# Weight sums of a seven-product matrix scheme: GpSimd differences of loaded tiles, or adding DMA transfers from DRAM

## The chip, the cores and the metric

The kernel runs on one core of a Trainium2 chip. The metric is the device time of one execution in microseconds (us), and a kernel is described by the median of its runs. A profiled execution gives a trace; times inside it are counted from the start of its span. In the traces PE is TensorE, DVE is VectorE, ACT is ScalarE, POOL is GpSimd and SP is SyncE, which here issues most of the DMA transfers.

## What is computed

One inference step of a transformer-like layer: a token mixer (attention and mLSTM) and then an MLP, for 640 tokens (512 latent and 128 context tokens) of width 1024. The change touches the MLP alone, and of it the first matrix:

```python
D_MODEL, D_FF = 1024, 4096

def trunk_layer(x, ...):
    ...
    x = x + gate1 * rmsnorm(mix, post1)
    h = rmsnorm(x, pre2) * (1 + scale2) + shift2
    ff = jnp.square(jax.nn.relu(h @ w_mlp1)) @ w_mlp2
    x = x + gate2 * rmsnorm(ff, post2)
```

All arithmetic is float32. On TensorE every product of two float32 matrices is made of three: each factor is split into a high and a low part (fp32r), and high x high, high x low and low x high are summed.

## The kernel before

Everything ahead of the MLP is left alone. The MLP works on transposed activations `h2`, 128 features by 640 tokens, eight such slabs. `w_mlp1` is cut into 32 blocks of 128 columns and `w_mlp2` accordingly; the loop `for ch in range(NCH)` takes four blocks a round. Chunk 0 makes plain products with tiles loaded early (`w0`). Chunks 1 to 7 take their four blocks as two pairs (`p`), and make h @ w_mlp1 for a pair with seven products in place of eight: the tokens are cut into two halves of 320, the 1024 features into two halves of 512, and the pair gives two column blocks. So the activations are a 2 x 2 block matrix A(i, j), the weights one of four quarters of 128 x 512 elements (256 KB), and a scheme of Strassen's kind needs sums of blocks on either side:

- the sums of the activation blocks, called S3 to S7 (`fac`, `parts`, L1055 to L1066), are made once, at the end of chunk 0, on DVE and GpSimd, and split into high and low parts by ACT and DVE;
- the sums of the weight quarters, made anew for each pair in `factors`. `raw_pair` loads both blocks (512 KB each) into the one tile `gate`. GpSimd makes from it `t13` and `t24`, two tiles of two quarters each (L845 to L849, four operations). They come from the pool entry `x2`, which has three buffers, so the second pair's `t24` reuses the buffer of the first pair's `t13` of the same chunk. `quarters` then splits a tile of two quarters into high and low parts: an ACT cast (L829) and a DVE subtraction (L830), into a ring of six weight tiles (`ring`) that also serves the `w_mlp2` tiles (`load_w`, L107 to L112). The lone fourth quarter goes into `mix` (L853, L854).

`pair` runs the products: the banks bY, bW and bV collect running sums, copied from bank to bank by ACT (L1009, L1015, L1022), and `squared` makes relu squared and splits the result into `uh` and `ul`, which the products with `w_mlp2` (L116 to L118, in `sums`) read.

The program is written in this order for each chunk, but a scheduler decides the order of the instructions on each engine, by a simulated timeline; each engine then works strictly in its order. `tc.issue_after(mark[...])` holds a group of instructions back in that planning until the marked one. All loads from DRAM here go through SP's queue, which waits at each transfer until its buffer is free; behind it the next transfers stand.

Of the kernel before, what the change touches and what calls it, by code (L numbers as in the profile page):

```python
# [26 lines left out]
def _build(ctx, tc, nc, a, dbg):  # L27
# [802 lines left out]
        V.tensor_tensor(out=lo, in0=x, in1=hi, op=ALU.subtract)  # L830
        return [[y.rearrange("p (q k n) -> p q k n", q=2, k=4)[:, q] for y in (hi, lo)] for q in range(2)]

    def raw_pair(src):
        raw = pR_.tile([P, 2, 1024], F32, name="gate")
        for n in range(2):
            nc.sync.dma_start(raw[:, n, :], src[n])
        return raw[:, 0, :], raw[:, 1, :]

    def factors(b1, b2, f):

        if 1 not in f:
            f[1], f[2] = quarters(b1)
        q1, q2 = ([b[:, 0:512], b[:, 512:1024]] for b in (b1, b2))
        t13 = pR_.tile([P, 1024], F32, name="x2", bufs=3)
        G.tensor_tensor(out=t13[:, 0:512], in0=q2[0], in1=q1[0], op=ALU.subtract)  # L845
        G.tensor_tensor(out=t13[:, 512:1024], in0=q2[1], in1=q2[0], op=ALU.subtract)
        t24 = pR_.tile([P, 1024], F32, name="x2", bufs=3)
        G.tensor_tensor(out=t24[:, 0:512], in0=q2[1], in1=t13[:, 0:512], op=ALU.subtract)
        G.tensor_tensor(out=t24[:, 512:1024], in0=q1[1], in1=t24[:, 0:512], op=ALU.subtract)  # L849

        v = pR_.tile([P, 1024], F32R, name="mix", bufs=2)
        hi, lo = v[:, 0:512], v[:, 512:1024]
        S.copy(hi, q2[1])  # L853
        V.tensor_tensor(out=lo, in0=q2[1], in1=hi, op=ALU.subtract)  # L854
        f[3] = [y.rearrange("p (k n) -> p k n", k=4) for y in (hi, lo)]

        def rest():
            f[5], f[7] = quarters(t13)
            f[6], f[4] = quarters(t24)
        return rest  # L860
# [129 lines left out]
    def squared(uh, ul, i, r=None, ps=None):  # L990

        c = slice(320 * i, 320 * i + 320)
        u = pF_.tile([P, 320], F32, name="u", bufs=2)
        if ps is not None:
            S.activation(out=u, in_=ps, func=AF.Relu)  # L995
            V.tensor_tensor(out=u, in0=u, in1=u, op=ALU.mult)  # L996
        else:
            V.scalar_tensor_tensor(out=u, in0=r, scalar=0.0, in1=r, op0=ALU.max, op1=ALU.mult)
        S.copy(uh[:, c], u)  # L999
        V.tensor_tensor(out=ul[:, c], in0=u, in1=uh[:, c], op=ALU.subtract)  # L1000

# [39 lines left out]
    for ch in range(NCH):  # L1041
        us = []
        if ch == 0:
            uu = [u_pair() for _ in range(2)]
            us = [(u[0][n], u[1][n]) for u in uu for n in range(2)]
            for hf in range(2):
                q = (f2[1], f2[2]) if hf == 0 else (f2[3], f2[4])
                for m in range(CH):
                    ps = bank1()[:, 0:320]
                    with tc.issue_after(mark["turn"]) if m == 3 and hf == 0 else ExitStack():  # L1050
                        for k in range(KD):
                            x = [y[:, k % 4, :] for y in q[k // 4]]
                            mm3(ps, w0[m][0][:, k, :], w0[m][1][:, k, :], *x, k == 0, k == KD - 1)
                    squared(*us[m], hf, ps=ps)
            for h, k in enumerate(ks):  # L1055
                V.tensor_tensor(out=s1[h], in0=A(1, 0)[:, k, :], in1=A(1, 1)[:, k, :], op=ALU.add)
                parts(5, h, s1[h])
            for h, k in enumerate(ks):
                mark["S2"] = G.tensor_tensor(out=s1[h], in0=s1[h], in1=A(0, 0)[:, k, :], op=ALU.subtract).ins
                parts(6, h, s1[h])  # L1060
            for h, k in enumerate(ks):
                G.tensor_tensor(out=A(1, 0)[:, k, :], in0=A(0, 0)[:, k, :], in1=A(1, 0)[:, k, :], op=ALU.subtract)
                parts(7, h, A(1, 0)[:, k, :])
            for h, k in enumerate(ks):
                V.tensor_tensor(out=A(0, 1)[:, k, :], in0=A(0, 1)[:, k, :], in1=s1[h], op=ALU.subtract)
                parts(3, h, A(0, 1)[:, k, :])  # L1066
        else:
            if ch == 1:
                weights(1, keep=1)
                banks(0, 5)  # L1070
                pfork = tc.tile_pool(name="pfork", bufs=1, space=bass.MemoryType.PSUM, reuse_waits="tile")
                pfork_ = pfork.__enter__()
                forks = [pfork_.tile([P, 512], F32, name="b" + s)[:, 0:320] for s in "YWV"]

                for b in forks:
                    prime(b)
            for p in range(2):
                n = ch * 2 + p
                f = {}
                with tc.issue_after(mark["S2"]) if n == 2 else ExitStack():  # L1080
                    rest = factors(*raw_pair(a["w_mlp1"][2 * n:2 * n + 2]), f)
                rest()
                u = u_pair()
                for _ in pair(f, False, u, [bank1()[:, 0:320] for _ in range(2)] + forks):
                    pass
                us += [(u[0][n], u[1][n]) for n in range(2)]
# [160 lines left out]
```

## Time and profile before

| | us |
|---|---|
| median of 3 runs (lowest, highest) | 1057.35 (1056.98, 1058.0) |
| profiled execution | 1055.42 |
| its span, first to last instruction | 1053.7 |
| PE busy in the span | 1022.7 (97%) |
| DVE, ACT, POOL busy | 561.0, 424.2, 238.1 |

Matmuls overlap their neighbours, so PE's busy share says that it hardly idled, not that it ran at its peak. The granted TensorE clock was 0.996 of full speed over the span. The page's cut into 40 slices shows TensorE at nine tenths or more in nearly all of them; the stretch in which the MLP begins, about 630 to 660 us, and the first and the last slice are the exceptions. The chain that ended last runs 89% through PE.

### The profile page before, as it was taken

The numbers are of one execution on the slowest core, as the hardware profiler recorded it, in microseconds if no ns is written. First come the engines' busy times: TensorE is split into PE (matmuls) and PEld (weight loads), VectorE is DVE, ScalarE is ACT, GpSimd is POOL, SyncE is SP. The second block draws the span as 40 slices with busy tenths as digits, with TensorE's granted clock in tenths as the row PEclk, the third lists the DMA queues.
The fourth block names the chain that finished last, engine by engine and source line by source line (L and its number), as shares of the span: only waits on it lengthen the run. The fifth ranks groups of instructions, "written<-read, shape, count | busy, mean of one in ns | idle before, by whom it ended". The sixth has DMA issues, their size and how long they took to land.

```text
span 1053.7 us, 15728 instructions
## 1 busy us (share of the span) xinstructions
PE 1022.7 (97%) x6342; PEld 907.0 (86%) x6342; DVE 561.0 (53%) x955; ACT 424.2 (40%) x784; POOL 238.1 (23%) x218
## 2 busy tenths in 40 slices
PE   4999999899999999999999998999999999999997
PEld 2899899888889888888888897898989898989896
DVE  4655255767664222222334489365566565656557
ACT  4354244277775222222223564442425152515142
POOL 3011225424560000001000015224040404040101
PEclk9999999999999999999999999999999999999999
DMA  9444132211002444444446251231313131313034
GB/s 372 168 129 145 46 109 73 75 41 41 15 8 79 139 143 140 141 140 141 140 141 223 77 180 62 79 121 40 120 40 120 40 120 41 121 41 121 1 111 169
DMA packets 40121, 112.03 MB, mean 106 GB/s; under 512 B 4280, under 2 KB 14168, under 8 KB 38768
## 3 DMA queue, kind: packets, MB, share of 16 engines
q1 hardware_dynamic: 34656, 92.92, 25.8%
q0 software_dynamic: 4672, 16.80, 4.9%
q10 hardware_dynamic: 720, 1.31, 0.3%
q8 instruction: 50, 0.82, 0.3%
q14 instruction: 23, 0.19, 0.1%
HBM read 105.03 MB, written 5.98 MB: 105 GB/s over the span
## 4 chain that ended last, share of the span: by engine, by line
PE 89%; DVE 5%; ACT 2%; issue 2%; DMA 1%; POOL 1%; SPq 0%; POOLq 0%; DVEq 0%; ACTq 0%
PE b L116 20%; PE b L117 20%; PE b L118 20%; PE b L937 7%; PE bY L937 5%; PE b L149 3%; PE bV L937 2%; PE bW L937 2%; PE b L695 2%; PE b L683 2%; PE b L229 1%; PE b L496 1%; PE b L470 1%; DMA x<-x 1%; DMA gate<-w_mlp 1%
## 5 line engine op out<-in xcount | busy, mean ns | idle before, releaser
L112 DVE TENSOR_TENSOR wl<-raw,wh 128x1024 fp32r<-128x1024 f32 (+2 forms) x67 | 80.5, 1202 | 157.7 <-ACT wh L111 156.4
L111 ACT CAST wh<-raw 128x1024 fp32r<-128x1024 f32 (+2 forms) x69 | 69.8, 1013 | 175.0 <-PE b L117 157.0
L117 PE MATMUL b<-h1l,wh 128*128 128x320 f32 x400 | 125.2, 313 | 0.0
L116 PE MATMUL b<-h1h,wh 128*128 128x320 f32 x384 | 119.9, 312 | 0.0
L118 PE MATMUL b<-h1h,wl 128*128 128x320 f32 x384 | 118.9, 310 | 0.0
L117 PEld LDWEIGHTS b<-h1l,wh 128*128 128x128 f32 x400 | 75.2, 188 | 6.9 <-issue 6.9
L116 PEld LDWEIGHTS b<-h1h,wh 128*128 128x128 f32 x384 | 72.2, 188 | 7.1 <-DVE sg L808 5.0
L845 POOL TENSOR_TENSOR x<-gate 128x512 f32<-128x512 f32 x14 | 19.7, 1406 | 235.2 <-DMA gate<-w_mlp 220.8
L118 PEld LDWEIGHTS b<-h1h,wl 128*128 128x128 f32 x384 | 72.2, 188 | 0.3 <-issue 0.2
L117 PE MATMUL b<-wlx,uh 128*128 128x512 f32 (+1 forms) x164 | 64.5, 393 | 2.4 <-DVE wlx L112 2.4
L116 PE MATMUL b<-whx,uh 128*128 128x512 f32 (+1 forms) x164 | 64.1, 395 | 1.6 <-ACT u L995 1.6
L1125 DVE TENSOR_TENSOR h1h<-h1h,b 128x512 f32<-128x512 f32 (+1 forms) x71 | 46.2, 673 | 35.8 <-PE b L118 35.6
L117 PE MATMUL b<-wl,uh 128*128 128x512 f32 x160 | 63.2, 395 | 0.0
L116 PE MATMUL b<-wh,uh 128*128 128x512 f32 x160 | 62.1, 396 | 0.0
L118 PE MATMUL b<-whx,ul 128*128 128x512 f32 (+1 forms) x164 | 61.5, 393 | 0.0
L118 PE MATMUL b<-wh,ul 128*128 128x512 f32 x160 | 60.4, 394 | 0.0
L742 POOL DMA_DIRECT2D aw<-w_ada x32 | 17.4, 545 | 185.8 <-PE b L149 178.6
L999 ACT CAST uh<-u 128x320 fp32r<-128x320 f32 x64 | 29.3, 459 | 74.4 <-DVE u L996 48.7
L612 POOL TENSOR_TENSOR pt<-pt,sm 128x640 f32<-128x640 f32 x32 | 40.0, 1255 | 46.7 <-DVE sm L610 44.5
L112 DVE TENSOR_TENSOR wlx<-raw,whx 128x1024 fp32r<-128x1024 f32 (+2 forms) x28 | 34.6, 1234 | 27.9 <-ACT whx L111 27.8
L149 PE MATMUL b<-aw,csil 128*32 128x256 f32 (+1 forms) x256 | 35.2, 519 | 6.4 <-DMA aw<-w_ada 6.4
L117 PEld LDWEIGHTS b<-wlx,uh 128*128 128x128 f32 x164 | 31.1, 190 | 9.6 <-DVE wlx L112 2.8
(432 smaller groups left out, 2812.8 us busy)
## 6 DMA issues: line engine op xcount, KB each, us to landing
raw<-w_mlp SPq DMA_DIRECT2D x36, 512.0 KB, 3.2
aw<-w_ada POOLq DMA_DIRECT2D x32, 512.0 KB, 4.2
gate<-w_mlp SPq DMA_DIRECT2D x28, 512.0 KB
aw<-w_ada SPq DMA_DIRECT2D x8, 1024.0 KB, 12.0
raw<-w_g SPq DMA_DIRECT2D x16, 512.0 KB, 5.3
x<-x SPq DMA_DIRECT2D x10, 512.0 KB, 8.0
raw<-w_y SPq DMA_DIRECT2D x8, 512.0 KB, 3.3
raw<-w_out SPq DMA_DIRECT2D x8, 512.0 KB, 4.3
```

Source lines behind the costliest of these rows:

```text
L111: S.copy(hi, raw)
L112: eng.tensor_tensor(out=lo, in0=raw, in1=hi, op=ALU.subtract)
L116: T.matmul(out, lh, rh, start=start, stop=False)
L117: T.matmul(out, lh, rl, start=False, stop=False)
L118: T.matmul(out, ll, rh, start=False, stop=stop)
L149: T.matmul(ps[32 * j:32 * j + 32, 0:n], csil[:, k, :], raws[k], start=k < 4, stop=k >= 4, tile_position=(0, 32 * j))
L612: G.tensor_tensor(out=pt, in0=pt, in1=sm.broadcast_to([P, 640]), op=ALU.mult)
L683: T.transpose(pp[:, j * 128:(j + 1) * 128], pt[:, j * 128:(j + 1) * 128], ident)
L695: T.matmul(pv[64 * e:64 * e + 64, 0:128], vn[:, j, h * 64:(h + 1) * 64], pT[:, j, e * 128:e * 128 + 128], start=j == 0, stop=j == 4, tile_ ...
L937: T.matmul(out, w[u][:, k, :], x[v][:, k, :], start=start and k == 0 and i == 0, stop=k == 3 and i == 2, skip_group_check=True)
L999: S.copy(uh[:, c], u)
L1125: V.tensor_tensor(out=o, in0=o, in1=ps, op=ALU.add)
```

## The change

`raw_pair` is gone and `factors` takes the two blocks in DRAM. The weight sums are no longer made by GpSimd instructions from the raw tile. SP loads a quarter into each half of `t13` and of `t24`, and then transfers of GpSimd's queue, with `accum_op=ALU.add`, add further quarters from DRAM to what stands in the tile: one to both halves of `t13`, two to both halves of `t24`, and one more to the second half of `t24`. Each of these waits for the one before on the same tile. The raw tile keeps block one and the fourth quarter (768 KB a pair in place of 1 MB). So a pair loads 1.75 MB through SP and 1.75 MB through GpSimd's queue, in place of 1 MB through SP.

An adding transfer can't subtract, so the signs of the activation sums are changed such that every weight sum is a plain sum: S5 becomes a difference, S6 and the later S3 are formed with the opposite sign by scalar_tensor_tensor on DVE (two halves each; S6 was GpSimd's), and one of the two column blocks comes out negated, so that its relu squared is made with min in place of max. The plan's mark for the first pair of chunk 1 moves from the GpSimd operation of S6 to that of S7.

```diff
@@ -830,28 +830,29 @@
         V.tensor_tensor(out=lo, in0=x, in1=hi, op=ALU.subtract)
         return [[y.rearrange("p (q k n) -> p q k n", q=2, k=4)[:, q] for y in (hi, lo)] for q in range(2)]
 
-    def raw_pair(src):
-        raw = pR_.tile([P, 2, 1024], F32, name="gate")
-        for n in range(2):
-            nc.sync.dma_start(raw[:, n, :], src[n])
-        return raw[:, 0, :], raw[:, 1, :]
-
-    def factors(b1, b2, f):
-
-        if 1 not in f:
-            f[1], f[2] = quarters(b1)
-        q1, q2 = ([b[:, 0:512], b[:, 512:1024]] for b in (b1, b2))
-        t13 = pR_.tile([P, 1024], F32, name="x2", bufs=3)
-        G.tensor_tensor(out=t13[:, 0:512], in0=q2[0], in1=q1[0], op=ALU.subtract)
-        G.tensor_tensor(out=t13[:, 512:1024], in0=q2[1], in1=q2[0], op=ALU.subtract)
-        t24 = pR_.tile([P, 1024], F32, name="x2", bufs=3)
-        G.tensor_tensor(out=t24[:, 0:512], in0=q2[1], in1=t13[:, 0:512], op=ALU.subtract)
-        G.tensor_tensor(out=t24[:, 512:1024], in0=q1[1], in1=t24[:, 0:512], op=ALU.subtract)
-
+    def factors(src, f):
+
+        q = lambda i, j: src[j][:, 512 * i:512 * i + 512]
+        two = lambda x: x.unsqueeze(1).broadcast_to([P, 2, 512])
+        raw = pR_.tile([P, 2048], F32, name="gate")[:, 0:1536]
+        nc.sync.dma_start(raw[:, 0:1024], src[0])
+        nc.sync.dma_start(raw[:, 1024:1536], q(1, 1))
+
+        sums = []
+        for x in ((q(0, 0), q(1, 1)), (q(1, 1), q(1, 0))):
+            sums.append(pR_.tile([P, 1024], F32, name="x2", bufs=3))
+            for h in range(2):
+                nc.sync.dma_start(sums[-1][:, 512 * h:512 * h + 512], x[h])
+        t13, t24 = sums
+        add = lambda out, x: G.dma_start(out, x, accum_op=ALU.add)
+        for t, x in ((t13, q(0, 1)), (t24, q(0, 1)), (t24, q(0, 0))):
+            add(t.rearrange("p (q n) -> p q n", q=2), two(x))
+        add(t24[:, 512:1024], q(1, 1))
+        f[1], f[2] = quarters(raw[:, 0:1024])
         v = pR_.tile([P, 1024], F32R, name="mix", bufs=2)
         hi, lo = v[:, 0:512], v[:, 512:1024]
-        S.copy(hi, q2[1])
-        V.tensor_tensor(out=lo, in0=q2[1], in1=hi, op=ALU.subtract)
+        S.copy(hi, raw[:, 1024:1536])
+        V.tensor_tensor(out=lo, in0=raw[:, 1024:1536], in1=hi, op=ALU.subtract)
         f[3] = [y.rearrange("p (k n) -> p k n", k=4) for y in (hi, lo)]
 
         def rest():
@@ -995,7 +996,7 @@
             S.activation(out=u, in_=ps, func=AF.Relu)
             V.tensor_tensor(out=u, in0=u, in1=u, op=ALU.mult)
         else:
-            V.scalar_tensor_tensor(out=u, in0=r, scalar=0.0, in1=r, op0=ALU.max, op1=ALU.mult)
+            V.scalar_tensor_tensor(out=u, in0=r, scalar=0.0, in1=r, op0=ALU.min, op1=ALU.mult)
         S.copy(uh[:, c], u)
         V.tensor_tensor(out=ul[:, c], in0=u, in1=uh[:, c], op=ALU.subtract)
 
@@ -1053,16 +1054,17 @@
                             mm3(ps, w0[m][0][:, k, :], w0[m][1][:, k, :], *x, k == 0, k == KD - 1)
                     squared(*us[m], hf, ps=ps)
             for h, k in enumerate(ks):
-                V.tensor_tensor(out=s1[h], in0=A(1, 0)[:, k, :], in1=A(1, 1)[:, k, :], op=ALU.add)
+                V.tensor_tensor(out=s1[h], in0=A(1, 1)[:, k, :], in1=A(1, 0)[:, k, :], op=ALU.subtract)
                 parts(5, h, s1[h])
             for h, k in enumerate(ks):
-                mark["S2"] = G.tensor_tensor(out=s1[h], in0=s1[h], in1=A(0, 0)[:, k, :], op=ALU.subtract).ins
+                V.scalar_tensor_tensor(out=s1[h], in0=s1[h], scalar=-1.0, in1=A(0, 0)[:, k, :], op0=ALU.mult, op1=ALU.subtract)
                 parts(6, h, s1[h])
             for h, k in enumerate(ks):
-                G.tensor_tensor(out=A(1, 0)[:, k, :], in0=A(0, 0)[:, k, :], in1=A(1, 0)[:, k, :], op=ALU.subtract)
+                mark["G"] = G.tensor_tensor(out=A(1, 0)[:, k, :], in0=A(0, 0)[:, k, :], in1=A(1, 0)[:, k, :],
+                                            op=ALU.subtract).ins
                 parts(7, h, A(1, 0)[:, k, :])
             for h, k in enumerate(ks):
-                V.tensor_tensor(out=A(0, 1)[:, k, :], in0=A(0, 1)[:, k, :], in1=s1[h], op=ALU.subtract)
+                V.scalar_tensor_tensor(out=A(0, 1)[:, k, :], in0=s1[h], scalar=-1.0, in1=A(0, 1)[:, k, :], op0=ALU.mult, op1=ALU.subtract)
                 parts(3, h, A(0, 1)[:, k, :])
         else:
             if ch == 1:
@@ -1077,8 +1079,8 @@
             for p in range(2):
                 n = ch * 2 + p
                 f = {}
-                with tc.issue_after(mark["S2"]) if n == 2 else ExitStack():
-                    rest = factors(*raw_pair(a["w_mlp1"][2 * n:2 * n + 2]), f)
+                with tc.issue_after(mark["G"]) if n == 2 else ExitStack():
+                    rest = factors(a["w_mlp1"][2 * n:2 * n + 2], f)
                 rest()
                 u = u_pair()
                 for _ in pair(f, False, u, [bank1()[:, 0:320] for _ in range(2)] + forks):
```

How the instructions stand, before and now, at three places. In these rows h1h is the buffer of `h2`, `mix` the tiles of the activation sums, `gate` the raw weight tiles and `x2` the tiles t13 and t24; names carry a number for each allocation.

GpSimd where chunk 0 ends and chunk 1 is prepared, before:

```order
L1062 TENSOR_TENSOR h1h_5534<-h1h_5534 128x2x320 x2
L1059 TENSOR_TENSOR mix_6021<-mix_6021,h1h_5534 128x640
L1059 TENSOR_TENSOR mix_6022<-mix_6022,h1h_5534 128x640
L845 TENSOR_TENSOR x2_6503<-gate_6496 128x512
L846 TENSOR_TENSOR x2_6503<-gate_6496 128x512
L848 TENSOR_TENSOR x2_6506<-gate_6496,x2_6503 128x512
L849 TENSOR_TENSOR x2_6506<-gate_6496,x2_6506 128x512
```

Two differences of activation blocks, two more, and the weight differences of the first pair. GpSimd at the same place, now (x2_6499 and x2_6502 are t13 and t24 of the first pair, x2_6644 and x2_6647 those of the second):

```order
L847 DMA x2_6644<-w_mlp1 128x2x512
L1063 TENSOR_TENSOR h1h_5534<-h1h_5534 128x2x320 x2
L847 DMA x2_6499<-w_mlp1 128x2x512
L847 DMA x2_6502<-w_mlp1 128x2x512 x2
L847 DMA x2_6502<-w_mlp1 128x512
L847 DMA x2_6647<-w_mlp1 128x2x512
L847 DMA x2_6953<-w_mlp1 128x2x512
L847 DMA x2_6647<-w_mlp1 128x2x512
L847 DMA x2_6647<-w_mlp1 128x512
```

Of the arithmetic the two operations of L1063 are left, one adding transfer stands ahead of them, and a transfer for the next chunk (x2_6953) stands between those of x2_6647.

ACT at the start of chunk 1, before (x2_6644 and x2_6647 are the second pair's t13 and t24):

```order
L829 CAST whx10_6657<-x2_6647 128x1024
L1123 COPY h1h_6041<-b1_6451 128x512
L829 CAST whx01_6640<-gate_6637 128x1024
L1123 COPY h1h_6041<-b1_6465 128x512
L829 CAST wh1_6653<-x2_6644 128x1024
L1009 COPY bY_6490<-b1_6524 128x320
L1015 COPY bW_6491<-bY_6490 128x320
L111 CAST wh2_6780<-raw_6778 128x1024
L995 ACTIVATE u_6576<-b1_6524 128x320
L999 CAST uh_6520<-u_6576 128x320
```

ACT at the same place, now:

```order
L829 CAST whx01_6654<-gate_6641 128x1024
L1125 COPY h1h_6041<-b1_6465 128x512
L829 CAST wh1_6661<-x2_6644 128x1024
L1010 COPY bY_6490<-b1_6528 128x320
L829 CAST whx10_6665<-x2_6647 128x1024
L1016 COPY bW_6491<-bY_6490 128x320
L111 CAST wh2_6788<-raw_6786 128x1024
L996 ACTIVATE u_6580<-b1_6528 128x320
L1000 CAST uh_6524<-u_6580 128x320
```

The cast of the second pair's t24 has moved four places back, behind the copy of bY and ahead of that of bW. In the later chunks ACT's order is what it was, the casts of the second pair's t13 and t24 ahead of the copy of bY.

SP around the start of a later chunk, before:

```order
L836 DMA gate_7975<-w_mlp1 128x1024 x2
L836 DMA gate_8280<-w_mlp1 128x1024 x2
L107 DMA raw_8128<-w_mlp2 128x1024
L107 DMA raw_8134<-w_mlp2 128x1024
L107 DMA raw_8562<-w_mlp2 128x1024
L107 DMA raw_8568<-w_mlp2 128x1024
```

And now:

```order
L838 DMA gate_8003<-w_mlp1 128x1024
L839 DMA gate_8003<-w_mlp1 128x512
L845 DMA x2_8009<-w_mlp1 128x512 x2
L845 DMA x2_8315<-w_mlp1 128x512 x2
L838 DMA gate_8312<-w_mlp1 128x1024
L839 DMA gate_8312<-w_mlp1 128x512
L845 DMA x2_8318<-w_mlp1 128x512 x2
L845 DMA x2_8460<-w_mlp1 128x512 x2
L107 DMA raw_8160<-w_mlp2 128x1024
```

Between the raw weight loads and ahead of the `w_mlp2` loads stand the quarter loads of four tiles: x2_8009 is t24 of the running chunk's second pair, the others belong to the next chunk. TensorE's order is the same before and now.

## Rows read from the trace of the kernel before

**Rows 1.** Busy by stretch: us, PE, PEld, DVE, ACT, POOL, clock, DMA share, GB/s.

```profile
632.00:660.00 28.00, 24.05 (x126) 20.77 (x125) 24.35 (x26) 13.72 (x23) 15.99 (x8) 0.94 0.23 73
924.00:977.00 53.00, 53.00 (x291) 47.47 (x290) 32.17 (x46) 18.81 (x30) 13.16 (x9) 1.00 0.23 80
...
650.00:653.50 3.50, 3.48 (x9) 2.17 (x7) 3.50 (x7) 2.48 (x5) 0.00 (x0) 0.52 0.72 215
660.00:677.50 17.50, 17.50 (x76) 14.08 (x76) 5.69 (x5) 8.04 (x11) 6.44 (x4) 1.00 0.09 35
```

**Rows 2.** Waits of PE, 540 to 670 us: us, times, longest.

```profile
PE b L117 <- DVE wlx L112: 2.4, 1, 2.4
PE b L116 <- ACT u L995: 1.6, 1, 1.6
```

**Rows 3.** Timeline of PE: start us, us, engine, line, operation, tile, idle before.

```profile
649.20 0.50 PE L117 MATMUL b<-wlx,uh 128*128 128x512 f32 x1 [2.37 <-DVE wlx L112]
...
655.40 0.39 PE L117 MATMUL b<-wlx,uh 128*128 128x512 f32 x1
655.63 0.40 PE L118 MATMUL b<-whx,ul 128*128 128x512 f32 x1
...
691.65 0.40 PE L116 MATMUL b<-wh,uh 128*128 128x512 f32 x1
```

**Rows 4.** Timeline of POOL, 618 to 680 us, first and last of six groups.

```profile
629.98 6.89 POOL L1062 TENSOR_TENSOR h1h<-h1h 128x640 f32<-128x640 f32 x2 [6.91 <-DVE S3l L979]
...
646.34 1.73 POOL L849 TENSOR_TENSOR x<-gate,x 128x512 f32<-128x512 f32 x1
```

**Rows 5.** Timeline of DVE, 618 to 680 us.

```profile
630.49 0.82 DVE L979 TENSOR_TENSOR S3l<-h1h,S3h 128x640 fp32r<-128x640 f32 x1
...
639.58 2.20 DVE L1065 TENSOR_TENSOR h1h<-h1h,mix 128x640 f32<-128x640 f32 x1
...
646.87 2.28 DVE L112 TENSOR_TENSOR wlx<-raw,whx 128x1024 fp32r<-128x1024 f32 x1
...
650.21 1.21 DVE L112 TENSOR_TENSOR wlx<-raw,whx 128x1024 fp32r<-128x1024 f32 x1
```

**Rows 6.** DVE's groups by shape, 660 to 1000 us: busy us, mean ns, idle.

```profile
L1000 DVE TENSOR_TENSOR ul<-u,uh 128x320 fp32r<-128x320 f32 x48 | 23.5, 490 | 10.3 <-ACT uh L999 9.5
...
L998 DVE SCALAR_TENSOR_TENSOR u<-r 128x320 f32<-128x320 f32 x24 | 11.7, 486 | 0.2
```

**Rows 7.** DMA, 340 to 540 us: packets, MB, share; issues with median to landing.

```profile
q0 software_dynamic: 4352, 15.74, 24.0%
...
aw<-w_ada POOLq DMA_DIRECT2D x30, 512.0 KB, 4.0
```

**Rows 8.** DMA issues of the whole span, the page's part 6.

```profile
raw<-w_mlp SPq DMA_DIRECT2D x36, 512.0 KB, 3.2
```

**Rows 9.** Timeline of DVE at the end of chunk 0.

```profile
669.10 1.22 DVE L830 TENSOR_TENSOR wl<-x,wh 128x1024 fp32r<-128x1024 f32 x1 [4.74 <-ACT wh L829]
```

**Rows 10.** Timeline of ACT, end of chunk 0 and end of chunk 3.

```profile
668.02 1.05 ACT L829 CAST wh<-x 128x1024 fp32r<-128x1024 f32 x1 [0.87 <-PE b L118]
...
815.25 1.05 ACT L829 CAST wh<-x 128x1024 fp32r<-128x1024 f32 x1
...
836.11 1.05 ACT L829 CAST whx<-x 128x1024 fp32r<-128x1024 f32 x1 [0.35 <-PE b L118]
837.82 0.41 ACT L1009 COPY bY<-b 128x320 f32<-128x320 f32 x1 [0.66 <-PE b L937]
```

**Rows 11.** The chain that ended last, merged: start us, us, what; chunk starts and bY.

```profile
677.73 5.14 PE b L937 x35
...
783.36 5.13 PE b L937 x35
...
836.01 5.13 PE b L937 x35
841.15 1.76 PE bY L937 x12
```

## Prediction

> **What bounds the kernel now.** I read the busy time by stretches first. From 660 us on the engine that ends last is TensorE: a 53 us stretch of the steady part has 53.00 us of matmul in it [rows 1], and no wait of TensorE is listed behind 670 us. There the change can gain nothing; it can only keep everything ready or fail to. What is not full is the turn into the MLP, 632 to 660 us: 24.05 of 28 us busy, at a granted clock of 0.94 [rows 1]. The list of TensorE's waits names two stalls there, 2.4 us on a low half that DVE writes (wlx, L112) and 1.6 us on an ACT evacuation (L995) [rows 2]. Behind the first stall TensorE runs at its lower level, 1.2 GHz, for a while: between 650 and 653.5 us the granted clock is 0.52 and nine matmuls take 3.48 us [rows 1]; at full clock they start 0.23 us apart [rows 3].
>
> Next, why DVE is late there. GpSimd works from 629.98 us without a break on two differences of activation blocks and then on the four weight differences of the first pair, up to 648 us [rows 4]. DVE's operations beside it are two to three times longer: the same width of 640 elements takes 0.82 us at 630.49 and 2.20 us at 639.58, and the low half that TensorE waits for takes 2.28 us where the next one, with GpSimd quiet, takes 1.21 [rows 5].
>
> **Term 1: the turn, a gain.** The change takes two of four 640-wide operations from GpSimd (L1059 goes to DVE as scalar_tensor_tensor) and all weight differences. GpSimd is then through its arithmetic near 636.9 us, the point where the first group ends in [rows 4]. DVE gets two operations more; a scalar_tensor_tensor of 320 elements costs 0.49 us, as a tensor_tensor does [rows 6], so at 640 about 0.8 us each, 1.6 in all. It gets back the excess of what stands beside GpSimd: 1.4 for L1065 and 1.1 for the low half in the rows shown [rows 5], about 7 us over the seven operations from 636 to 649 us that repeat the pattern. In DVE's new order I put the low half's end near 643 us; TensorE wants it at 646.8 (649.20 less its wait of 2.37 [rows 3]). That stall goes. The second, 1.6 us [rows 2], stands behind a weight tile whose load waits for this same low half to free its buffer; it moves forward by some 5 us with it. With no idle stretch ahead of it the clock should stay at 2.4 GHz, which gives back 3.48 − 9 x 0.23 = 1.4 us. Sum 2.37 + 1.6 + 1.4 = 5.4 us. What is late next is the release of a PSUM bank by L996, which in my count comes within a microsecond of TensorE's new pace, so I take 4.9, with ends 0 and 5.4. Swapped signs, max for min and a load 256 KB shorter per pair have nothing to cost: same sizes, other work above them.
>
> Moved issues: GpSimd's queue now begins this stretch with an adding transfer ahead of L1063. It waits for a load that SP can issue only after the store of the last x2 tile; I get a landing near 628 us, and GpSimd waits until 629.98 anyway, for DVE [rows 4]. Cover 2 us; past that L1063, the S7 casts behind it and DVE are late one for one. SP's early quarter loads stand ahead of w_mlp loads that wait for DVE in any case, so I cost them at nothing.
>
> **Term 2: the chain of t24 of the second pair, a loss.** Before, GpSimd made all four quarters from one raw tile within 8 us. Now t24 is load, add, add, half add, each waiting for the one before to land. Its tile (three buffers) comes free only when DVE has finished the low half of t13 of the first pair in the same chunk. So seven times, once a chunk, a chain starts late by construction: it runs from that low half to ACT's cast of the second pair's t24.
>
> No row shows an adding transfer. The nearest are the GpSimd queue's plain loads of 512 KB: 4.0 us from issue to landing, of which, at 272 packets an engine in 24.0% of 200 us for 30 such loads, 1.6 us are data [rows 7]. The low bound of an add is that plain 4.0 us (3.2 for 256 KB, half the data); it can't be lower, since the same bytes come from DRAM. The high bound is two whole transfers end to end: 8.0 and 6.4, as if the destination were fetched in a pass of its own. I take the fixed part once and the data twice, since two operands have to be read: 5.6, 5.6 and 4.0, together 15.2 us. That is nearer the low row, because engines that already stream packets need no second start. By the Trainium skill ("DMA: Bandwidth & Descriptors", Anatomy of one DMA) a transfer on this queue costs 2.0 us plus its bytes at 436 GB/s; with both operands counted as bytes that would be, as an estimate, 4.4, 4.4 and 3.2 us, 12.0 together, and the loss below would be 0.6 us and the slow clock at most. The plain loads speak against so small a fixed part: 4.0 us [rows 7] where that rule gives 3.2.
>
> The two quarter loads ahead are 512 KB from SP: 3.2 us [rows 8] and 0.4 for the second issue, 3.6.
>
> *First chunk.* The low half of t13 ends at 669.10 + 1.22 = 670.3 [rows 9]; its cast at 668.02 waited for TensorE [rows 10], so in step with TensorE it stays there relative to the chunk's start at 677.73 [rows 11]. The change's other transfers beside the chain (a load and an add for the next chunk, 768 KB of raw weights) share the same engines; they carry about as many bytes as two adds and overlap half of it: 2 us. Ready at 670.3 + 3.6 + 15.2 + 2 = 691.1. Needed: in ACT's new order the cast stands ahead of the copy of bW, a raw cast, a relu and, over DVE's square, uh. With 0.95 + 0.36 + 0.95 + 0.43 + 0.48 + 0.46 us and 0.2 at four hand-overs that is 4.4 us up to uh, which TensorE reads at 691.65 [rows 3]; so the cast has to start by 687.3. Late by 3.8 us; a stall of that length has cost another 1.4 us of slow clock above. Loss 5.2, with ends 0 (all adds at the plain 11.2 us, no sharing: ready at 685.1) and 12.4.
>
> *Six later chunks.* The cast of t13 starts at 815.25 [rows 10], when TensorE has let go of its ring tile; without GpSimd beside it its low half ends near 817.6. Ready at 817.6 + 3.6 + 15.2 + 1.5 for the raw load and the next t13 load beside it = 837.9. The cast stood at 836.11 and the copy of bY behind it [rows 10] must be done before TensorE starts bY at 841.15 [rows 11]: 841.15 − 0.2 − 0.41 − 0.95 = 839.6. Margin 1.7 us, cost nothing. Everything else in the ring has room: t13 of either pair needs one add and has over 20 us, t24 of the first pair over 30.
>
> **The sum.** The profiled execution took 1055.42 us, span 1053.7. 1055.4 − 4.9 + 5.2 = 1055.7. The median of the runs, 1057.35, stands 1.93 us above the profiled execution, so 1057.6: what the turn gives, the first chain takes. A change of 0.2%, about 2.1 us, is what a measurement of this kernel can tell from none.
>
> **Rivals.**
> *Quick adds.* If the three adds together stay under 687.3 − 670.3 − 3.6 − 2 = 11.4 us, the first chain is in time and only the gain is left: 1050.5, or 1052.4 on the runs' scale, 1051.9 with the full 5.4. For it: between 660 and 677.5 us the DMA engines are busy 0.09 of the time [rows 1], so the chain may share less than I think. Against it: a plain 512 KB already takes 4.0, and the second operand is more bytes. The page's rule above would land here.
>
> *The later chains miss.* The margin of 1.7 us is used up when the three adds take over 16.9 us. Then ACT, which works in order, holds the copy of bY behind the cast, TensorE stalls in each of six chunks, and each stall can bring the slow clock with it. With 19 us for three adds: 2.1 + 1.4 in each of six, 7.6 + 1.4 in the first, less 4.9: +25, so 1082. With the high bound of 22.4 us 1106; just past the point 1060. For it: four transfers in series for what GpSimd did in 6 to 8 us, in rows of half the length (2 KB). Against it: the data part would have to be nearly two and a half times the plain one.
>
> *The turn keeps its stalls.* GpSimd's own queue is held by the early adding transfer or DVE still stands beside busy GpSimd, while the first chain is late all the same: 1055.4 + 5 and up, 1062. The rows of the contention [rows 5] speak against it.
>
> **How the numbers follow.** Forecast (gain and loss cancel, own range 1054.5 to 1060) 0.40; quick adds 0.27; later chains miss 0.28; turn keeps its stalls 0.05. The range takes the forecast, most of the first rival and the lower half of the second: 1051.8 to 1082, leaving out some 0.2. Faster: 0.26 of quick adds and 0.09 of the forecast, 0.35. Same: 0.26 of the forecast, 0.01 and 0.03 of the first two rivals' near ends, 0.30. Slower: 0.05 + 0.25 + 0.05 = 0.35.
>
> **What will show it.** Right: no wait of TensorE on wlx L112 near 646 us and a granted clock near 1.00 in that stretch; DVE's 640-wide operations at 0.8 us; one new stall near the first bW product with ACT waiting for an adding transfer of t24; no TensorE wait in the six later chunks; adds of 512 KB landing in 5 to 6 us. Wrong: ACT waiting for t24 in each chunk and a chunk longer than the 52.65 us between two starts of now [rows 11] (three adds over 16.9 us), or no stall at all in the first (three adds under 11.4).

## The result, and the profile after

The changed kernel takes 1073.38 us at the median of four runs (1070.38 to 1077.49), the kernel before 1057.16 on the same chip (four runs): 1.0155 times the time, with an interval of 1.0119 to 1.0191. It is slower, by 16 us. That lies inside the range, but it is not the forecast of 1057.6; it is the second rival, "the later chains miss". The profiled execution of the changed kernel took 1077.49 us, its span 1075.6, 21.9 more than before.

Busy time of the changed kernel by stretch, columns as in [rows 1]:

```profile
632.00:660.00 28.00, 28.00 (x155) 25.04 (x154) 20.78 (x30) 16.13 (x28) 10.51 (x6) 1.00 0.80 183
660.00:713.00 53.00, 45.72 (x244) 41.18 (x243) 21.79 (x31) 19.96 (x32) 9.04 (x8) 0.94 0.74 178
713.00:766.00 53.00, 53.00 (x292) 47.44 (x290) 29.24 (x44) 18.67 (x30) 9.04 (x8) 1.00 0.73 172
766.00:819.00 53.00, 50.31 (x279) 45.03 (x277) 27.98 (x42) 18.18 (x29) 9.11 (x8) 1.00 0.73 171
819.00:871.00 52.00, 49.26 (x259) 43.95 (x258) 24.62 (x38) 15.06 (x24) 8.18 (x7) 0.97 0.69 165
...
924.00:977.00 53.00, 50.07 (x260) 44.35 (x260) 25.76 (x39) 15.85 (x25) 9.05 (x8) 0.97 0.70 165
```

The first line answers to that of [rows 1] for the same stretch: 24.05 us busy at a clock of 0.94 have become 28.00 at 1.00. The turn gained what it was to gain: the first chunk's products begin 50.25 us behind GpSimd's last small operation ahead of the MLP (rs_x at 623.40), where they began 55.22 behind it (677.57 and 622.35), 5.0 us. From 660 us on the full stretches of before have holes in TensorE's column, and the DMA share (the last but one) is near 0.7, where the steady line of [rows 1] has 0.23. The waits of TensorE from 600 us on (us in total, times, longest) name the holes:

```profile
PE bY L938 <- ACT bY L1010: 12.3, 5, 2.9
PE bY L938 <- ACT bW L1016: 6.6, 1, 6.6
PE b L938 <- ACT h1h L1125: 0.7, 1, 0.7
```

Both waits of [rows 2] are gone. In their place stand 6.6 us in the first chunk and five of 1.7 to 2.9 us later, and ACT is the engine named. Together 18.9 us. The rest of the loss is the clock behind them. The 24 matmuls behind the first wait take 3.57 and 2.38 us, twelve each, where twelve take 1.76 at full clock: 2.4 us. (The 0.94 over 53 us would be 3.2, but part of that fall lies inside the wait: 0.73 from 687.20 to 690.70.) In each of the two 0.97 stretches 0.03 is 1.6 us. Together 5.6. Less the 5.0 us of the turn that is 19.5 of the 21.9 us; another 1.1 arose ahead of the MLP, by the two times of rs_x above.

ACT is only the messenger. The chain that ended last, followed back from the wait at 796.21 (start, us, what):

```profile
770.38 1.24 DVE wlx L830
...
771.64 0.33 SPq L845
...
772.02 3.19 DMA x<-w_mlp
...
775.77 5.35 DMA x<-w_mlp
...
781.41 1.20 POOL x L847
782.62 7.58 issue
...
790.22 4.41 DMA x<-w_mlp
...
794.79 1.04 ACT wh L829
795.83 0.34 ACT bY L1010
...
796.21 2.03 PE bY L938 x12
```

This reads downwards as one buffer's life: DVE finishes the low half of t13 of the first pair, SP loads the quarters of t24 of the second pair into that buffer, then come three adds (5.6 us from start to start; 8.8, of which the trace records the end as 7.58 of "issue"; 4.4), the cast, the copy of bY, and TensorE. In the first chunk the same chain runs from 665.55 to the cast at 689.37, with adds of 5.9, 10.0 and 3.8 us. Of the page's DMA issues (KB each, median us from issue to landing), two answer to [rows 7, 8]:

```profile
x<-w_mlp POOLq DMA_DIRECT2D x42, 512.0 KB, 7.4
raw<-w_mlp SPq DMA_DIRECT2D x36, 512.0 KB, 3.9
```

### The profile page after: what moved, and what is told of

The parts are those of the page before. It is cut to its first block, busy times and chain, and to the rows that moved or that the text cites. A ratio compares the mean times of both kernels' runs of the same rounds, so it can differ in the third digit from the quotient of the medians.

```text
span 1075.6 us, 15897 instructions
## 1 busy us (share of the span) xinstructions
PE 1028.1 (96%) x6342; PEld 911.5 (85%) x6342; DVE 538.3 (50%) x957; ACT 423.4 (39%) x784; POOL 207.1 (19%) x216
## 4 chain that ended last, share of the span: by engine, by line
PE 68%; DMA 14%; issue 6%; DVE 5%; ACT 4%; POOL 1%; SPq 0%; POOLq 0%; DVEq 0%; ACTq 0%
PE b L116 16%; PE b L118 16%; PE b L117 16%; DMA x<-w_mlp 8%; PE bY L938 4%; PE b L938 3%; DMA raw<-w_mlp 3%; PE b L149 3%; PE b L695 2%; DMA gate<-w_mlp 2%; PE b L229 1%; PE b L683 1%; PE bW L938 1%; PE bV L938 1%; DVE wl L112 1%
## 5 line engine op out<-in xcount | busy, mean ns | idle before, releaser
L847 POOL DMA_DIRECT2D x<-w_mlp x56 | 63.5, 1199 | 320.0 <-DMA x<-w_mlp 295.0
L111 ACT CAST whx<-raw 128x1024 fp32r<-128x1024 f32 (+2 forms) x28 | 28.8, 1029 | 28.1 <-DMA raw<-w_out 9.3
```

The lines of the kernel that those rows point to most:

```text
L111: S.copy(hi, raw)
L847: add = lambda out, x: G.dma_start(out, x, accum_op=ALU.add)
```

## The experiments

Theory: the turn gains some 5 us because GpSimd stops working on loaded tiles beside DVE; the loss is the serial chain of t24 of the second pair, whose buffer comes free late, and whose adds are slow because plain loads share the engines. Rivals: the added bytes slow everything; S6 on DVE alone is the turn's gain; the form of the transfers, not the adding, is slow. Each ratio is against the kernel before on the same chip.

| run | median us | ratio to before (95%) | TensorE's waits over 1 us, from 632 us |
|---|---|---|---|
| changed kernel | 1073.38 | 1.0155 (1.0119 to 1.0191) | 6.6, then five of 1.7 to 2.9 |
| e_swap | 1061.82 | 1.0035 (1.0024 to 1.0047) | 5.4 at the turn |
| e_swap2 | 1065.22 | 1.0059 (1.0044 to 1.0074) | 1.9 and 8.2 at the turn |
| e_swap3 | 1061.25 | 1.0026 (1.0015 to 1.0037) | 6.9 in the first chunk |
| e_turn | 1058.49 | 1.0004 (0.9996 to 1.0013) | 3.2 at the turn |
| e_s6pool | 1054.99 | 0.9970 (0.9956 to 0.9983) | 1.8 at the turn |
| e_hybrid | 1053.20 | 0.9958 (0.9945 to 0.9971) | none |
| e_plain | 1057.68 | 0.9994 (0.9985 to 1.0003) | 3.1 in the first chunk |
| e_noraw | 1059.55 | 1.0011 (0.9998 to 1.0024) | 4.8 in the first chunk |
| e_oneless | 1060.40 | 1.0020 (1.0010 to 1.0030) | 4.8 in the first chunk |
| e_onemore | 1123.05 | 1.0610 (1.0590 to 1.0630) | six of up to 9.3, one of 8.9 |

**The second pair's sums in the other order (e_swap).**

```diff
-        for x in ((q(0, 0), q(1, 1)), (q(1, 1), q(1, 0))):
-            sums.append(pR_.tile([P, 1024], F32, name="x2", bufs=3))
+        for j in ((1, 0) if f.get(0) else (0, 1)):
+            x = ((q(0, 0), q(1, 1)), (q(1, 1), q(1, 0)))[j]
+            sums[j] = pR_.tile([P, 1024], F32, name="x2", bufs=3)
...
-        for t, x in ((t13, q(0, 1)), (t24, q(0, 1)), (t24, q(0, 0))):
+        for j in ((1, 0) if f.get(0) else (0, 1)):
+            for x in (q(0, 1), q(0, 0))[:1 + j]:
...
-                f = {}
+                f = {0: p}
```

> The changed kernel with the two sums of the second pair in the other order: t24 is loaded and added first, into the buffer that is free early, and t13, with one add, takes the buffer that comes free late. Same transfers, same bytes, same casts. Theory (the serial chain of t24 in the late buffer makes the stalls, 6.6 us once and 2 to 3 us in most later chunks, and the clock falls behind them): the late chain is now a load of 3.6 us and one add of 5.6 to 7.4 us, 9 to 11 us where some 16 us are to be had, so no wait on bW or bY, the clock 1.00 from 713 on, and the turn's gain of 4 to 5 us is left: 1052 to 1054 us. Rival (the added traffic itself, 0.70 to 0.74 busy share of the DMA engines, slows whatever is loaded): the bytes are the same, so stalls stay somewhere, and 1065 to 1075 us. Second rival (adds of 8 to 10 us make even one add too late in the first chunk): one stall of 1 to 4 us at the first chunk, 1054 to 1058 us.

Measured 1061.82, in none of the three ranges. Every stretch from 713 to 977 us is full at clock 1.00, with all bytes still moving (DMA share 0.73 to 0.79): the added traffic alone doesn't stall the chunks. But the time is 8 us over what I expected, and the wait sits where the turn was free before:

```profile
658.70 0.80 PE L116 MATMUL b<-whx,uh 128*128 128x512 f32 x1 [5.42 <-ACT u L999]
```

GpSimd's timeline of the same run shows one cause:

```profile
639.47 1.21 POOL L848 DMA_DIRECT2D x<-w_mlp  x1 [6.05 <-DMA x<-w_mlp]
640.24 3.57 POOL L1066 TENSOR_TENSOR h1h<-h1h 128x640 f32<-128x640 f32 x2
```

The second pair's t24 now takes the free buffer, so two of its adds stand ahead of S7 on GpSimd, the second waits 6.05 us for the first, and S7 begins at 640.24 where the changed kernel has it at 631.16.

**The same, held back until S7 is formed (e_swap2).**

```diff
-                with tc.issue_after(mark["G"]) if n == 2 else ExitStack():
+                with tc.issue_after(mark["G"]) if n <= 3 else ExitStack():
```

> The version with the second pair's t24 ahead of its t13, and with the second pair's transfers of the first chunk also held back until GpSimd has formed S7. In the version without that hold two of that pair's adds stood ahead of S7 in GpSimd's order, the second waited 6.05 us for the first, S7 began at 640.24 instead of 631 to 632, and TensorE waited 5.42 us for u at 658.70. Theory (the chunks are cured by the order, and the rest was this wait): S7 begins at 631 to 633, no PE wait of over 1 us from 632 to 977, clock 1.00 in 632:660 and in each later stretch: 1052.5 to 1054.5 us. Rival (the added traffic makes the turn late anyway, as the raw loads took 4.9 us at the median where they take 3.3 in the kernel without adds): a wait of 2 to 5 us stays at the turn or at the first chunk: 1057 to 1061 us.

Measured 1065.22, worse and above both ranges, though S7 began at 633.01 as it should. My theory of the 5.4 us was too small. ACT's timeline:

```profile
667.03 1.04 ACT L829 CAST whx<-x 128x1024 fp32r<-128x1024 f32 x1 [12.23 <-DMA x<-w_mlp]
667.98 0.43 ACT L999 ACTIVATE u<-b 128x320 f32<-128x320 f32 x1
```

With its buffer free early, the cast of that t24 has also moved up in ACT's order, ahead of the relu u of the turn, and waits 12.23 us for adds that share GpSimd's queue with the first pair's. A tile made early was cast early, in front of work that was due.

**The other order from the second chunk on only (e_swap3).**

```diff
-                f = {0: p}
+                f = {0: p * (n > 3)}
```

> The version with the second pair's t24 ahead of its t13, with the first chunk left in the order of the changed kernel. (With that order in the first chunk too, ScalarE's cast of the second pair's t24 stood ahead of the casts and evictions of the turn and waited for its adds: 4.1 us idle at 653.40 in one version, 12.2 us at 667.03 in the other.) Theory: the turn is as in the changed kernel (no wait, clock 1.00 in 632:660), the first chunk keeps its wait on bW of 5 to 7 us with a clock of 0.94 behind it, the later chunks have none: 1053 plus 6.6 plus 3.2, 1060 to 1064 us. Rival (first chunk and later chunks are coupled, the later ones start late and stay late): waits of 1 to 3 us in some later chunks, 1065 to 1070 us.

Measured 1061.25, as the theory has it: no wait at the turn, 6.9 us on bW, clock 0.94 from 660 to 713 us, the stretches behind it full but for 0.28 us. So the order of two sums over three buffers, from the second chunk on, is worth 12 us (1073.38 less 1061.25; the kernel before took 1057.16 beside the one and 1058.30 beside the other).

**One add fewer, one more (e_oneless, e_onemore).** Both change the sum t24, the one by leaving out a summand, the other by adding one twice.

```diff
-        for t, x in ((t13, q(0, 1)), (t24, q(0, 1)), (t24, q(0, 0))):
+        for t, x in ((t13, q(0, 1)), (t24, q(0, 1))):
```

> The changed kernel with the second add of t24 (512 KB, q(0,0) into both halves) left out, so t24 lacks one summand. Theory (the stalls are the length of the late chain beyond what the schedule leaves): the chain of a later chunk loses 8 to 10 us of some 22 and ends 5 us or more before it is needed, so no wait on bY in the later chunks; the first chunk's wait on bW, 6.6 us, loses about the 10 us of that add and is gone, or under 1 us: 1052 to 1055 us. Rival (the stalls come from the load on the DMA engines): the bytes of the adds fall by two sevenths only, and at least half of the stalls stay: 1060 to 1067 us.

```diff
         add(t24[:, 512:1024], q(1, 1))
+        add(t24[:, 512:1024], q(1, 1))
```

> The changed kernel with the last add of t24 (256 KB into its right half) done twice, so that half has one summand too many. Theory (the late chain of the second pair sets the time of each chunk): seven chunks are later by one more add each, 4 to 5 us, and chunk 2, which hardly waits now, by 2 to 4 us; 26 to 34 us in all, and some 2 to 6 us more for stretches at the lower clock behind the waits: 1099 to 1112 us. Rival (load on the DMA engines, total bytes): 256 KB more in fourteen chains are 3.7 MB on 42.5 MB in the queue of the adds, so under 3 us: 1073 to 1077 us.

Without the add no later chunk waits; with the extra one six waits on bY come to 43.4 us, and the time rises by 50 us, not by the 26 to 39 I had: 256 KB more in each of fourteen chains. Total bytes can't do that; the length of the chain can. The size was off both ways. In the one, an add more is also 256 KB more beside the other adds (512 KB at 8.0 us, where the changed kernel has 7.4), and the granted clock is 0.90 to 0.94 in five of the six stretches from 660 to 977. In the other, 4.8 us stay in the first chunk, with a clock of 0.94 over the stretch. They are on bY now: the plan has put ACT's cast of that t24 ahead of the copy of bY there, so the edit moved an order too. So its 1060.40 lies in the range that I had given to the rival, whose later stalls didn't come.

**The transfers without adding (e_plain).** The sums are left out, the last transfer overwrites.

```diff
-        add = lambda out, x: G.dma_start(out, x, accum_op=ALU.add)
+        add = lambda out, x: G.dma_start(out, x)
```

> The changed kernel with the adding transfers as plain transfers of the same sources, sizes, order and queue: the sums are left out, the last transfer overwrites. Theory (it is the accumulation that makes 512 KB last 7.4 us, where plain loads of 512 KB take 3.9 to 4.6 us): a transfer of 4 to 5.5 us from issue to landing, three in a row 12 to 15 us, under the 16.9 us that are to be had, so no stall in the later chunks and at most 2 us at the first: 1052 to 1056 us. Rival (the form of the transfer, pieces of 2 KB issued by GpSimd at 1.2 us each, is what is slow): still 6 to 8 us each, the stalls stay, 1065 to 1075 us.

Measured 1057.68, above the range of the theory and far below the rival's. The same four transfers in a row no longer make later chunks wait; 3.1 us stay in the first. DMA from 713 to 977 us, the adding queue's packets, MB and share of 16 engines, and the issues, of the changed kernel:

```profile
q0 software_dynamic: 9130, 17.49, 40.6%
...
x<-w_mlp POOLq DMA_DIRECT2D x30, 512.0 KB, 7.7
```

and of the one without adding:

```profile
q0 software_dynamic: 5120, 18.35, 21.1%
...
x<-w_mlp POOLq DMA_DIRECT2D x30, 512.0 KB, 4.8
```

Adding nearly doubles the engines' time for the same bytes (40.6 against 21.1%) and takes a transfer from 4.8 to 7.7 us. A plain transfer of this form, 2 KB rows with a source read twice, takes 4.8 us against the 4.0 of [rows 7], at a DMA share of 0.54 to 0.56 against 0.42; which of the two makes the difference no run tells.

**Fewer plain loads beside the adds (e_noraw).** From the third pair on the raw tiles of the first two are used again, so those pairs have three factors of the wrong blocks.

```diff
+        if len(kept) < 2:
+            kept.append(pR_.tile([P, 2048], F32, name="gate")[:, 0:1536])
             nc.sync.dma_start(kept[-1][:, 0:1024], src[0])
             nc.sync.dma_start(kept[-1][:, 1024:1536], q(1, 1))
+        raw = kept[-1]
```

> The changed kernel with the raw tiles (the blocks that are split without a sum, 768 KB a pair) loaded for the first two pairs only and used again by the later ones, so the later pairs have three factors of the wrong blocks. The chains of adds stay as they are; from the third pair on 768 KB of plain loads fewer share the DMA engines with them. Theory (an add of 512 KB takes 5.6 us undisturbed and 8 to 10 us when plain loads run beside it, and this is what carries the late chain over its limit): the second add of t24 in the chunks from 713 on falls from 8.8 to 9.7 us to 6 to 7 us, the chain by 2 to 3 us, and the waits on bY there, 1.8 to 2.9 us each, to under 0.5 us; the first chunk's wait stays at 4 to 7 us: 1060 to 1065 us. Rival (the second add is slow for itself, or because the next chain's adds share its queue): the waits on bY stay at 2 to 3 us: 1070 to 1077 us.

Measured 1059.55, a little under the range of the theory. GpSimd's timeline in one chunk (the second add begins in the first line shown, the third in the second):

```profile
777.85 1.20 POOL L849 DMA_DIRECT2D x<-w_mlp  x1 [4.46 <-DMA x<-w_mlp]
784.29 0.90 POOL L849 DMA_DIRECT2D x<-w_mlp  x1 [5.24 <-DMA x<-w_mlp]
```

and in the changed kernel:

```profile
781.41 1.20 POOL L847 DMA_DIRECT2D x<-w_mlp  x1 [4.44 <-DMA x<-w_mlp]
790.22 2.13 POOL L847 DMA_DIRECT2D x<-w_mlp  x2 [7.60 <-DMA x<-w_mlp]
```

The second add takes 6.4 us where it took 8.8, and no later chunk waits. In the changed kernel the next pair's raw tile, 768 KB that SP issues from 782.36 us, 1 us behind that add, runs beside it. But e_noraw also takes away the raw load ahead of the chain. ACT has nothing to wait for but TensorE when it casts t13:

```profile
765.74 1.05 ACT L829 CAST whx<-x 128x1024 fp32r<-128x1024 f32 x1 [1.24 <-PE bV L941]
```

so the chain begins 18.4 us ahead of its chunk (768.07, chunk at 786.44), where it has 16.6 in the changed kernel (771.62, chunk at 788.23). The wait to be removed was 2.7 us; the earlier start gains 1.8 and the faster add 2.4. The raw loads carry the chain past its limit, and by both ways; neither is shown to do it alone. So the rival "traffic" is right in this: by making the chain later and longer, not by slowing TensorE's other inputs.

**The turn taken apart (e_turn, e_s6pool, e_hybrid).** e_turn has the new signs and S6 on DVE, but GpSimd forms the four sums from the raw tile as before. e_hybrid forms t13 by the adding transfer and t24 on GpSimd from t13 and the raw tile. e_s6pool is e_hybrid with S6 back on GpSimd, with the other sign, so its sixth factor is not the scheme's.

```diff
+        G.dma_start(t13.rearrange("p (q n) -> p q n", q=2), two(q(0, 1)), accum_op=ALU.add)
+        G.tensor_tensor(out=t24[:, 0:512], in0=raw[:, 1024:1536], in1=t13[:, 0:512], op=ALU.add)
+        G.tensor_tensor(out=t24[:, 512:1024], in0=raw[:, 512:1024], in1=t24[:, 0:512], op=ALU.add)
```

> The changed kernel's signs with the sums on GpSimd as before (four additions of the loaded tile instead of four subtractions, no adding transfer): S6 is formed on VectorE, GpSimd forms S7 and the weight sums. Theory (the turn's gain is from S6 leaving GpSimd, not from GpSimd being free of the weight sums): no PE wait on the w_mlp2 factors near 646 and clock 1.00 in 632:660, the later chunks as in the kernel before, 1052 to 1054 us. Rival (the gain at the turn needs the weight sums off GpSimd too, since their time beside VectorE slows its sums): the wait of about 2.4 us stays, 1056 to 1058 us.

> The changed kernel with only t13 formed by an adding transfer; t24 is formed on GpSimd from t13 and the raw tile, by two additions of 512 columns. Theory: no chain of adds is left (one add of 5.6 to 7.4 us, two additions on GpSimd of about 1.2 us each), no stall in the chunks, the turn's gain stays: 1052 to 1054 us, the same as with the order of the second pair turned round. Rival (any adding transfer in the chunks costs, by traffic or by GpSimd's issue): 1056 to 1062 us.

```diff
-                V.scalar_tensor_tensor(out=s1[h], in0=s1[h], scalar=-1.0, in1=A(0, 0)[:, k, :], op0=ALU.mult, op1=ALU.subtract)
+                mark["S2"] = G.tensor_tensor(out=s1[h], in0=s1[h], in1=A(0, 0)[:, k, :], op=ALU.add).ins
```

> The version with only t13 formed by an adding transfer and t24 on GpSimd (1053.2 us), with S6 back on GpSimd as in the kernel before (two additions of 640 columns, with the other sign, so the sixth factor is not the one that the scheme wants). Theory from the runs so far (VectorE's sums are slow at the turn while GpSimd works on loaded tiles, whatever that work is): S6 on GpSimd takes from 637 to 641 beside VectorE, 4 us, where the four weight sums of the kernel before took 7 more; VectorE's S3 and the wlx parts behind it are then done 1 to 3 us later, TensorE waits for u 1 to 2 us: 1054.5 to 1056.5 us. Rival (S6 on VectorE is nothing, the weight sums off GpSimd are the whole gain at the turn): 1053 to 1054 us. Second rival (S6 off GpSimd is the whole gain): 1057 to 1058.5 us.

S6 on DVE alone gives nothing that can be measured (1058.49): my theory for e_turn fell, and a wait stayed, 3.2 us where its rival had 2.4. The weight sums moved and S6 left on GpSimd give 3 us (1054.99), both 5 (1053.20). Moved means here that GpSimd forms only t24's sums and begins with them over 5 us later: 19.9 us behind rs_x in e_hybrid and 14.6 in e_turn, 24.3 in e_s6pool and 18.7 in the kernel before. In e_turn, GpSimd puts the sums where S6 was:

```profile
637.77 1.87 POOL L845 TENSOR_TENSOR x<-gate 128x512 f32<-128x512 f32 x1
```

and DVE beside it takes 3.75 us for two operations:

```profile
638.41 3.75 DVE L1059 SCALAR_TENSOR_TENSOR mix<-mix,h1h 128x640 f32<-128x640 f32 x2
```

which in e_hybrid, with GpSimd issuing a transfer and waiting for it at that time, take 1.55:

```profile
639.83 1.55 DVE L1057 SCALAR_TENSOR_TENSOR mix<-mix,h1h 128x640 f32<-128x640 f32 x2
```

e_hybrid beats both kernels, the one before by 0.4% (interval 0.29 to 0.55). It keeps the turn's gain and has no chain: t24 needs two additions of 1.4 us where three adds stood. From 713 to 977 us TensorE is busy in every microsecond at clock 1.00, and the DMA share is 0.41 to 0.42.

## Why the prediction was right and wrong, step by step

**What bounds the kernel, and term 1.** Right. TensorE is full from 713 to 977 us in every version without a late chain, but for 0.28 us in e_swap3. The stalls and the slow clock of the turn went: 5.0 us up to the first chunk's start, for 4.9, of which a new wait of 0.7 us on h1h (an eviction by ACT) is already taken off; I had put what is late next on another PSUM bank, L996's. DVE's 640-wide operations from 637 us on take 0.81 us, but for one of 1.43. The contention of [rows 5] is what the runs point to (3.75 us in e_turn, 1.55 in e_hybrid, for the same two operations). One row didn't show it: the 0.82 us at 630.49 also stand beside a working GpSimd (L1062 from 629.98). The quiet case of the same kernel is this:

```profile
649.48 0.81 DVE L979 TENSOR_TENSOR S6l<-mix,S6h 128x640 fp32r<-128x640 f32 x1
```

That moving two operations to DVE is worth nothing while GpSimd goes on with the weight sums, the sum couldn't show, since it took both at once. The early adding transfer cost nothing: S7 began 0.21 us behind DVE's release of it. One more such transfer there held S7 back by 6 us (e_swap).

**Term 2, the first chunk.** Right in kind, 6.6 us where I had 3.8. In times from the chunk's start: the chain began 0.7 us earlier than I had (−8.1, not −7.4), the load took 4.1 for 3.6, and the adds 5.9 + 10.0 + 3.8 = 19.7 for 15.2 + 2 of sharing. 3.8 − 0.7 + 0.5 + 2.5 = 6.1. The clock fell as in [rows 1] but for longer: 0.50 from 690.70 to 694.20 and 0.80 over the next 3.5 us (0.99 before), and 2.4 us lost behind the wait, for which I had 1.4.

**Term 2, the later chunks: the step that failed.** I gave them a margin of 1.7 us and cost them at nothing. From the chain above, with its chunk starting at 788.23:
- The chain began 16.6 us ahead of the chunk's start, not 18.4: 1.8 us. ACT's cast of t13 stood behind the cast of the raw tile, and that waited for its load:

```profile
768.77 0.62 ACT L854 CAST mix<-gate 128x512 fp32r<-128x512 f32 x1 [3.19 <-DMA gate<-w_mlp]
769.30 1.05 ACT L829 CAST whx<-x 128x1024 fp32r<-128x1024 f32 x1
```

  I had taken the start from before and put it down to TensorE alone. The kernel before has the same order, and there too the cast of the raw tile waited for its load, right ahead of the 815.25 of [rows 10]:

```profile
814.73 0.62 ACT L853 CAST mix<-gate 128x512 fp32r<-128x512 f32 x1 [2.39 <-DMA gate<-w_mlp]
```

  That is 21.3 us ahead of its chunk; 768.77 is 19.5 ahead. A later raw load makes a later chain, which I hadn't seen.
- The load took 4.1 us for 3.6: 0.5 us.
- The adds took 18.9 us (5.6, 8.8 and 4.4, from 775.77 to 794.63), for 15.2 + 1.5: 2.2 us.

4.5 us against 1.7 makes 2.8 us late; TensorE waited 2.69. The price of an add by itself was good: 5.6 us taken, 5.6 measured for the first. What was mis-sized most is sharing: I gave it 1.5 us for the whole chain, and the second add alone lost 2.4 to it (8.8 against 6.4 in e_noraw). I counted only the bytes that the neighbours move, at the plain price, and saw only the idle engines of [rows 1]; but each of the neighbours that adds keeps the engines twice as long, so a share of 0.23 became 0.7, where the same transfers without adding make it 0.54 to 0.56 (e_plain).

By the Trainium skill ("DMA: Bandwidth & Descriptors", Anatomy of one DMA), with both operands counted as bytes, the three adds would be 12.0 us, an estimate. The trace disagrees: 18.9, and 14.4 even if the second were as short as the first and the third took the 3.2 of that rule. The prediction says of this estimate that it would land with the quick adds; by its own sum 12.0 misses their 11.4 by 0.6 us. That rival fell in any case.

**The rivals.** "The later chains miss" named the place, the point (three adds over 16.9 us; 18.9 came) and the sign in the trace, ACT holding the copy of bY. Its 1082 had six later stalls with the slow clock behind each. Five came, and only two were followed by a lower clock (0.60 from 851.90 and 0.69 from 963.90; 1.00 behind the other three, over 3.5 us each), and the median run is 4 us below the profiled one. The time lies in the stated range because the range took in half of this rival; the forecast's own sum isn't borne out by that. Giving this rival 0.28 and the forecast 0.40 rested on the margin of 1.7 us, which had three estimates in it, all of which erred the same way.

## What to carry to other kernels

A sum made by adding transfers is a chain in series, each link of which waits for the one before to land, so give the longest chain the buffer that comes free first, and check in the recorded order of the casting engine that its early tile isn't cast in front of work that is due. Price a margin with the loads that the change itself starts beside the chain, since they are what fills engines that the old trace shows idle. Where one add replaces a difference and the rest can be formed on chip, mix the two: here one add and two short additions kept the gain of 5 us that the three further adds gave back four times over.

## What the runs showed of the hardware that was not expected

- An adding transfer holds GpSimd longer than a plain one of the same shape: 1.2 us an issue in the changed kernel, 0.7 without adding (the page's groups of L847: 1199 and 681 ns).
- GpSimd and DVE slow each other both ways. DVE gives way in [rows 5] and in e_turn, GpSimd here: S7's two operations take 6.89 us at 631.16 in the changed kernel, with DVE busy for 4.6 of them, and 3.57 at 640.24 in e_swap, where DVE had waited since 638 (spans on GpSimd are rough). In e_hybrid GpSimd's first addition for t24 is recorded with 10.95 us from 644.69, and DVE's 640-wide operations beside it stay at 0.81. Which of the two gives way was not settled.
- A wait of 2.7 to 2.9 us doesn't always bring the lower clock: behind the one of 2.69 at 796.21 it stayed at 1.00, behind the one of 2.75 at 851.89 it was 0.60 over 3.5 us. What decides between them stays open.
- Open: a fourth buffer for these tiles, the other way to start the chain early, was not tried.
